# A four-layer streaming encoder step on eight cores: layer order, folded pool matrix, and the convolution as banded matmuls

## The chip, the cores and the metric

The kernel runs on all 8 cores of one Trainium2 chip. Each core computes one prompt stream of 4096 frames and four of 32 short streams of 32 frames; the cores exchange nothing. The time is the device time of the slowest core, in microseconds (us). The runs here fall into two states. In the fast one all cores agree within about 1%. In the slow one the cores of a die, or of both, show a lower granted TensorE clock and run some per cent longer (in the slow run of the kernel after one die took 4432.5 to 4500.5 us at clock 0.845 to 0.847, the other 4151.3 to 4173.9 us at 0.939 to 0.942).

## The reference

The model is 1024 wide, each branch 2048. Four layers: pool, conv, gating, pool.

```python
def rmsnorm(x, g): ...
def pool_mixer(u, hist, offset, w_grp, scale):
    # trailing-window means over 2, 4, 8, 16 frames, one window per 512 channels
    ...
    d = mean - u
    y = jnp.einsum('btgc,gcd->btgd', d, w_grp).reshape(B, T, E) * scale   # 512x512 group matrix
def conv_mixer(a, hist, w, b, ng, nb):
    # causal depthwise convolution, 31 taps, then LayerNorm and silu
    ...
def sgu_mixer(u, v, ws, bs, ng, nb):
    # LayerNorm of v, lower-triangular mix over 128 positions per head, y = u * s
    ...
for i in range(4):                      # pool, conv, gating, pool
    h = rmsnorm(x, norm_g[i])
    p = h @ in_w                        # 2E columns for pool, 3E for the others
    ...                                 # y = mixer(...)
    x = x + (y * jax.nn.silu(z)) @ out_w
return rmsnorm(x, final_g), ...         # and the last history rows of each layer
```

## The kernel before

It takes a group of 512 tokens (four of the eight groups carry 32 sample tokens too) through all four layers before it takes the next, and streams all weights from DRAM in each pass:

```python
for g in range(ngroups):                # 8 passes
    load_x(g)
    pool_layer(G, g, ...)
    conv_layer(G, g, ...)
    sgu_layer(G, g, ...)
    pool_layer(G, g, ...)
    rmsnorm(...)                        # final norm, store
```

The first pass loads each weight tile as f32 and casts it on ScalarE; it then stores the bf16 tile for the later passes:

```python
if grp == 0:
    S.add("sp", lambda e: [e.dma_start(out=stg[:, st, :], in_=wst[ci])], ...)
    S.add("act", lambda e: e.activation(out=slots[:, sl, :], in_=stg[:, st, :], func=AF.Copy), ...)
    S.add("act", lambda e: [e.dma_start(out=wq[ci], in_=slots[:, sl, :])], ...)
else:
    S.add("sp", lambda e: [e.dma_start(out=slots[:, sl, :], in_=wq[ci])], ...)
```

The convolution is split by taps. TensorE takes 19 of them (`NPE`), each as a matmul with a 128x128 diagonal; VectorE takes 12 as multiply-adds on the accumulator (the first of them, not shown, also fetches TensorE's sum from PSUM; the loop below does the other eleven):

```python
for k in range(NPE):                                   # pe_taps: TensorE
    for bi, (c0, n) in enumerate(cblocks):
        inst = e.matmul(psap(tAcc, bi, n), lhsT=dg[:, ...], rhs=agb[:, p, k + c0:k + c0 + n], ...)
...
ks = list(range(NPE + 1, 31))                          # rest: VectorE
for i, k in enumerate(ks):
    for ct in cts:
        S.add("dve", lambda e: e.scalar_tensor_tensor(
            out=big[:, ct, 0:Wc], in0=seqb[:, q, k:k + Wc], scalar=wcol,
            in1=big[:, ct, 0:Wc], op0=ALU.mult, op1=ALU.add), ...)
```

Of the kernel before, what the change touches and what calls it, by code (L numbers as in the profile page):

```python
# [11 lines left out]
D = 1024  # L12
# [5 lines left out]
TP = 512  # L18
NG = SEQ // TP
NCH = 120  # L20
NSLOT = 9
PF = 6
# [3 lines left out]
BIGW = 512 + 30 + 32  # L26
SEQW = 512 + 60 + 32

P_NORMG = 0
P_FINALG = P_NORMG + 32  # L30
P_PSCALE = P_FINALG + 8
P_CONVW = P_PSCALE + 32
P_CONVB = P_CONVW + 496
P_CONVNG = P_CONVB + 16
P_CONVNB = P_CONVNG + 16
NPAR = P_CONVNB + 16
B_SGG = 0
B_SGB = B_SGG + 2048
B_BSB = B_SGB + 2048
B_MASK = B_BSB + 512  # L40
B_RATIO = B_MASK + 128
B_IDENT = B_RATIO + 64
NBC = B_IDENT + 128
PINGPONG = True
NPE = 19

class Op:
    __slots__ = ("eng", "fn", "deps", "mark", "markno", "dkey", "dval", "idx", "tag")

class Sched:  # L50
    def __init__(self):
        self.ops = []
        self.last_w = {}
        self.readers = {}
        self.dcount = {}
        self.tag = None

    def add(self, eng, fn, reads=(), writes=(), dkey=None, ndma=1):
        op = Op()
        op.eng, op.fn, op.mark, op.markno, op.dkey, op.dval = eng, fn, False, 0, dkey, 0  # L60
        op.idx = len(self.ops)
        op.tag = self.tag
        deps = set()
        for k in reads:
            w = self.last_w.get(k)
            if w is not None:
                deps.add(w)
        for k in writes:
            w = self.last_w.get(k)
            if w is not None:  # L70
                deps.add(w)
            for r in self.readers.get(k, ()):
                deps.add(r)
        wset = set(writes)
        for k in writes:
            self.last_w[k] = op
            self.readers[k] = []
        for k in reads:
            if k not in wset:
                self.readers.setdefault(k, []).append(op)  # L80
        deps.discard(op)
        op.deps = deps
        if dkey is not None:
            self.dcount[dkey] = self.dcount.get(dkey, 0) + ndma
            op.dval = 16 * self.dcount[dkey]
        self.ops.append(op)
        return op

def build_program(depth=4, ngroups=NG):
    nc = bass.Bass("TRN2", target_bir_lowering=False)  # L90
    S = Sched()

    def dram(name, shape, dt, kind):
        return nc.dram_tensor(name, shape, dt, kind=kind).ap()

    xT = dram("xT", [8, 128, SEQ + NSAMP * SLEN], F32, "ExternalInput")
    wst = dram("wst", [NCH, 128, 2048], F32, "ExternalInput")
    params = dram("params", [128, NPAR], F32, "ExternalInput")
    bcin = dram("bcin", [128, NBC], F32, "ExternalInput")
    sgwT = dram("sgwT", [128, 4, 128], F32, "ExternalInput")  # L100
    stpool = dram("stpool", [2, NSAMP, 128, 240], F32, "ExternalInput")
    stconv = dram("stconv", [NSAMP, 128, 480], F32, "ExternalInput")
    yT = dram("yT", [8, 128, SEQ + NSAMP * SLEN], F32, "ExternalOutput")
    o_poolp = dram("o_poolp", [2, 128, 240], F32, "ExternalOutput")
    o_pools = dram("o_pools", [2, NSAMP, 128, 240], F32, "ExternalOutput")
    o_convp = dram("o_convp", [128, 480], F32, "ExternalOutput")
    o_convs = dram("o_convs", [NSAMP, 128, 480], F32, "ExternalOutput")
    o_sgup = dram("o_sgup", [128, 2048], F32, "ExternalOutput")
    o_sgus = dram("o_sgus", [NSAMP, SLEN, 2048], F32, "ExternalOutput")
    wq = dram("wq", [NCH, 128, 2048], BF16, "Internal")  # L110
    dgq = dram("dgq", [16, 128, NPE * 128], BF16, "Internal")

    es = ExitStack()

    def sb(name, shape, dt):
        return es.enter_context(nc.sbuf_tensor(name, shape, dt))

    ps = es.enter_context(nc.psum_tensor("ps", [128, 4096], F32))
    x = sb("x", [128, 8, 544], F32)
    h = sb("h", [128, 8, 544], BF16)  # L120
    ym = sb("ym", [128, 16, 544], BF16)
    big = sb("big", [128, 16, BIGW], F32)
    slots = sb("slots", [128, NSLOT, 2048], BF16)
    stg = sb("stg", [128, 2, 2048], F32)
    par = sb("par", [128, NPAR], F32)
    bc = sb("bc", [128, NBC], F32)
    sgw32 = sb("sgw32", [128, 4, 128], F32)
    wmT = sb("wmT", [128, 4, 128], BF16)
    ones_d = sb("ones_d", [128, 128], BF16)
    ones_e = sb("ones_e", [128, 128], BF16)  # L130
    epsb = sb("epsb", [128, 2], F32)
    pool_hp = sb("pool_hp", [128, 2, 16, 15], F32)
    conv_hp = sb("conv_hp", [128, 16, 30], F32)
    st_pool = sb("st_pool", [128, 2, 240], F32)
    st_conv = sb("st_conv", [128, 480], F32)
    pso = sb("pso", [128, 2, 240], F32)
    cso = sb("cso", [128, 480], F32)
    seqb = sb("seqb", [128, 4, SEQW], F32)
    sA = sb("sA", [128, SEQW], F32)
    sB = sb("sB", [128, SEQW], F32)  # L140
    dbuf = sb("dbuf", [128, 4, 544], BF16)
    dbuf2 = dbuf[:, :, :].rearrange("p a b -> p (a b)")
    t32 = sb("t32", [128, 2, 544], F32)
    t16 = sb("t16", [128, 2, 544], BF16)
    rs = sb("rs", [128, BIGW], F32)
    vraw = sb("vraw", [128, 2048], F32)
    bst = sb("bst", [128, 2, 24], F32)
    agb = sb("agb", [128, 2, SEQW], BF16)
    ident_bf = sb("ident_bf", [128, 128], BF16)
    ym2d = ym[:, :, :].rearrange("p a b -> p (a b)")  # L150
    DGOFF = [0, 5 * 544]
    dg = ym2d
    stg2d = stg[:, :, :].rearrange("p a b -> p (a b)")
    DGK = [[("ym", c) for c in range(0, 5)], [("ym", c) for c in range(5, 10)]]
    assert NPE * 128 <= 5 * 544
    dgs = vraw[:, :].bitcast(BF16)
    vrawB = ym2d[:, 0:4096].bitcast(F32)
    vnbB = ym2d[:, 4096:6144]
    assert tuple(vrawB.shape) == (128, 2048), vrawB.shape
    mv = sb("mv", [128, 2, 4], F32)  # L160

    state = {"tile": 0, "loaded": 0, "par": 0, "fine": 0}

    def next_tile(G):
        n = len(G["tiles"])
        t = state["tile"] % n
        state["tile"] = (t + 1) % n
        return G["tiles"][t]

    def psap(tile, bi, n, p0=0, p1=128, off=0):  # L170
        b = tile[bi]
        return ps[p0:p1, b * 512 + off: b * 512 + off + n]

    def PK(tile):
        return [("psb", b) for b in tile]

    def gstruct(g):
        even = (g % 2 == 0)
        if even:
            return dict(T=544, segs=[(0, 512), (512, 32)], blocks=[(0, 272), (272, 272)], s=g // 2,  # L180
                        tiles=[(0, 1), (2, 3), (4, 5)], aux=(6, 7), xi=0, g=g)
        return dict(T=512, segs=[(0, 512)], blocks=[(0, 512)], s=None,
                    tiles=[(b,) for b in range(7)], aux=(7,), xi=(1 if PINGPONG else 0), g=g)

    def XAP(G, k, c0, n):
        if G["xi"] == 0:
            return x[:, k, c0:c0 + n]
        return stg2d[:, k * 512 + c0:k * 512 + c0 + n]

    def XK(G, k):  # L190
        return ("x", k) if G["xi"] == 0 else ("xo", k)

    def pieces(G, c0, n, H):
        out = []
        for si, (s0, sn) in enumerate(G["segs"]):
            lo, hi = max(c0, s0), min(c0 + n, s0 + sn)
            if lo < hi:
                seqoff = H + (0 if si == 0 else 512 + H) + (lo - s0)
                cloff = (0 if si == 0 else 512 + H) + (lo - s0)
                out.append((lo, hi - lo, seqoff, cloff))  # L200
        return out

    def issue_load(gi):
        ci = gi % NCH
        grp = gi // NCH
        sl = gi % NSLOT
        if grp == 0:
            st = gi % 2
            S.add("sp", lambda e, ci=ci, st=st: [e.dma_start(out=stg[:, st, :], in_=wst[ci])],
                  reads=[], writes=[("stg", st)], dkey=("stg", st))  # L210
            S.add("act", lambda e, st=st, sl=sl: e.activation(out=slots[:, sl, :], in_=stg[:, st, :], func=AF.Copy),  # L211
                  reads=[("stg", st)], writes=[("slot", sl)])
# [5 lines left out]

    total_chunks = ngroups * NCH

    def use_chunk(gi, hold_from=None):
        upto = min(gi + PF, total_chunks - 1)
        if hold_from is not None:
            upto = min(upto, hold_from + NSLOT - 1)
# [862 lines left out]
```

## Time and profile before

| | before |
|---|---|
| runs | 5867.57, 5870.03 (fast), 6044.85, 6302.73 (slow) |
| TensorE busy | 4602 us, 78% |
| VectorE busy | 3348 us, 57% |
| granted TensorE clock, by core's die | 0.889 and 0.888 |

"Busy" for TensorE includes matmuls at half clock, so it is not work at the full rate: on core 7, the slowest, the 3.20 us from 1240.7 us on, at a granted clock of 0.50, touch 9 matmuls of 512 columns, the 3.40 us from 1244.1 us on, at 1.00, touch 18.

### The profile page before, as it was taken

The numbers are of one execution on the slowest core, as the hardware profiler recorded it, in microseconds if no ns is written. First come the engines' busy times: TensorE is split into PE (matmuls) and PEld (weight loads), VectorE is DVE, ScalarE is ACT, GpSimd is POOL, SyncE is SP. The second block draws the span as 40 slices with busy tenths as digits, with TensorE's granted clock in tenths as the row PEclk, the third lists the DMA queues.
The fourth block names the chain that finished last, engine by engine and source line by source line (L and its number), as shares of the span: only waits on it lengthen the run. The fifth ranks groups of instructions, "written<-read, shape, count | busy, mean of one in ns | idle before, by whom it ended". The sixth has DMA issues, their size and how long they took to land.

```text
span 5874.6 us, 89444 instructions; the slowest of 8 cores (5853.6 to 5874.6 us)
## 1 busy us (share of the span) xinstructions
PE 4602.0 (78%) x28896; PEld 2847.9 (48%) x28896; DVE 3348.4 (57%) x5365; ACT 1642.2 (28%) x3070; POOL 914.8 (16%) x1632
## 2 busy tenths in 40 slices
PE   3576667687898778987898878888798867998787
PEld 2454445233446556632436656733345646753343
DVE  2357415466465863658455765558646585466745
ACT  4434344213122142213222131221322122221312
POOL 3302011001111111201112121200112011210110
PEclk7787889898999889998999889999899979999888
DMA  6564587332443214432344222343243312443232
GB/s 223 216 219 129 172 290 245 130 117 77 136 142 117 83 60 148 140 120 85 113 148 138 98 79 96 127 143 109 86 148 133 113 62 92 140 138 123 90 114 97
DMA packets 208039, 768.82 MB, mean 131 GB/s; under 512 B 30432, under 2 KB 33888, under 8 KB 191840
## 3 DMA queue, kind: packets, MB, share of 16 engines
q1 hardware_dynamic: 188000, 690.23, 36.3%
q10 hardware_dynamic: 19584, 72.88, 3.0%
q8 instruction: 242, 3.96, 0.3%
q14 instruction: 213, 1.74, 0.1%
HBM read 668.29 MB, written 94.73 MB: 130 GB/s over the span
## 4 chain that ended last, share of the span: by engine, by line
PE 49%; DVE 19%; issue 13%; ACT 8%; DMA 6%; POOL 3%; ACTq 0%; DVEq 0%; SPq 0%; POOLq 0%
PE ps L242 30%; PE ps L513 11%; DMA stg<-wst 5%; DVE big L540 3%; PE ps L254 3%; PE ps L698 2%; DVE rs L290 2%; ACT slots L211 2%; DVE sA L375 2%; DVE sB L380 1%; DVE sA L384 1%; PE ps L306 1%; POOL ym L652 1%; DVE dbuf L400 1%; DVE h L292 1%
## 5 line engine op out<-in xcount | busy, mean ns | idle before, releaser
L242 PE MATMUL ps<-h,slots 128*128 128x272 bf16 (+1 forms) x13056 | 2031.0, 316 | 265.9 <-ACT big L413 112.3
L242 PEld LDWEIGHTS ps<-h,slots 128*128 128x128 bf16 x13056 | 1280.9, 99 | 994.7 <-issue 313.9
L540 DVE SCALAR_TENSOR_TENSOR big<-seqb,par,big 128x574 f32<-128x574 f32 (+1 forms) x1408 | 987.8, 782 | 0.0
L513 PE MATMUL ps<-agb,ym 128*128 128x287 bf16 (+1 forms) x3648 | 663.8, 349 | 205.4 <-ACT agb L489 201.2
L242 PE MATMUL ps<-ym,slots 128*128 128x272 bf16 (+1 forms) x5376 | 809.3, 313 | 2.2 <-DVE x L314 2.2
L242 PEld LDWEIGHTS ps<-ym,slots 128*128 128x128 bf16 x5376 | 525.2, 98 | 280.5 <-issue 3.2
L513 PEld LDWEIGHTS ps<-agb,ym 128*128 128x128 bf16 x3648 | 383.0, 106 | 485.6 <-issue 279.6
L365 ACT ACTIVATE seqb<-ps 128x272 f32<-128x272 f32 (+3 forms) x512 | 172.4, 392 | 760.1 <-PE ps L242 231.5
L423 DVE SCALAR_TENSOR_TENSOR ym<-ps,par,big 128x272 bf16<-128x272 f32 (+1 forms) x384 | 212.5, 582 | 297.2 <-PE ps L242 287.6
L369 POOL COPY pool_hp<-seqb 128x15 f32<-128x15 f32 x256 | 151.5, 592 | 1436.9 <-ACT seqb L365 1436.9
L698 PE MATMUL ps<-slots,h 128*128 128x256 bf16 (+1 forms) x2304 | 278.6, 286 | 91.8 <-DVE h L292 91.8
L791 DVE TENSOR_TENSOR t<-ps,t 128x272 f32<-128x272 f32 (+1 forms) x192 | 94.7, 522 | 438.2 <-ACT t L788 438.2
L794 POOL TENSOR_TENSOR ym<-t,big 128x544 bf16<-128x544 f32 (+1 forms) x128 | 154.7, 1209 | 1185.9 <-DVE t L791 1185.9
L314 DVE TENSOR_TENSOR x<-ps,x 128x272 f32<-128x272 f32 x256 | 100.4, 436 | 403.2 <-PE ps L242 310.7
L242 PE MATMUL ps<-dbuf,slots 128*128 128x272 bf16 (+1 forms) x1536 | 261.3, 330 | 79.4 <-DVE dbuf L400 76.7
L467 ACT ACTIVATE t<-ps 128x272 f32<-128x272 f32 (+1 forms) x192 | 82.1, 462 | 855.2 <-PE ps L242 855.1
L254 PE MATMUL ps<-h,slots 128*128 128x272 bf16 (+1 forms) x768 | 211.7, 424 | 136.8 <-DVE h L292 118.9
L375 DVE TENSOR_TENSOR sA<-seqb 128x573 f32<-128x573 f32 (+1 forms) x256 | 187.2, 731 | 206.6 <-ACT seqb L365 194.6
L698 PEld LDWEIGHTS ps<-slots,h 128*128 128x128 bf16 (+1 forms) x2304 | 234.5, 102 | 132.1 <-issue 94.0
L652 POOL TENSOR_TENSOR ym<-big,t 128x512 bf16<-128x512 f32 x192 | 207.3, 1107 | 495.3 <-ACT big L644 492.8
L211 ACT ACTIVATE slots<-stg 128x2048 bf16<-128x2048 f32 x120 | 229.5, 1912 | 172.3 <-DMA stg<-wst 162.1
L314 DVE TENSOR_TENSOR stg<-ps,stg 128x512 f32<-128x512 f32 x128 | 88.0, 691 | 327.3 <-PE ps L242 288.5
(97 smaller groups left out, 4146.6 us busy)
## 6 DMA issues: line engine op xcount, KB each, us to landing
slots<-wq SPq DMA_DIRECT2D x840, 512.0 KB, 3.8
stg<-wst SPq DMA_DIRECT2D x120, 1024.0 KB, 8.1
ym<-dgq SPq DMA_DIRECT2D x128, 608.0 KB, 4.1
wq<-slots ACTq DMA_DIRECT2D x120, 512.0 KB, 8.1
yT<-big SPq DMA_DIRECT2D x64, 256.0 KB, 3.0
dgq<-vraw ACTq DMA_DIRECT2D x16, 608.0 KB, 2.8
x<-xT SPq DMA_DIRECT2D x32, 256.0 KB, 5.5
stg<-xT SPq DMA_DIRECT2D x32, 256.0 KB, 2.8
```

Source lines behind the costliest of these rows:

```text
L211: S.add("act", lambda e, st=st, sl=sl: e.activation(out=slots[:, sl, :], in_=stg[:, st, :], func=AF.Copy), reads=[("stg", st)], writes=[(" ...
L242: inst = e.matmul(psap(tile, bi, n), lhsT=lhs_fn(k), rhs=rhs_fn(k, c0, n), start=(k == 0), stop=(k == nk - 1))
L254: inst = e.matmul(psap(tile, bi, n), lhsT=slots[:, sl, k * 256 + m2 * 128: k * 256 + m2 * 128 + 128], rhs=h[:, k, c0:c0 + n], start=(k == ...
L314: blockwise("dve", G, lambda e, bi, c0, n, m=m, tile=tile: e.tensor_tensor(out=XAP(G, m, c0, n), in0=psap(tile, bi, n), in1=XAP(G, m, c0, ...
L365: inst = e.activation(out=seqb[:, p, so:so + ln], in_=psap(tile, bi, ln, off=lo - c0), func=AF.Copy)
L375: S.add("dve", lambda e, p=p: e.tensor_tensor(out=sA[:, 1:W], in0=seqb[:, p, 1:W], in1=seqb[:, p, 0:W - 1], op=ALU.add), reads=[("seqb", p ...
L423: blockwise("dve", G, lambda e, bi, c0, n, ct=ct, tile=tile: e.scalar_tensor_tensor(out=ym[:, ct, c0:c0 + n], in0=psap(tile, bi, n), scala ...
L513: inst = e.matmul(psap(tAcc, bi, n), lhsT=dg[:, DGOFF[p] + k * 128:DGOFF[p] + (k + 1) * 128], rhs=agb[:, p, k + c0:k + c0 + n], start=(k = ...
L540: S.add("dve", lambda e, q=q, ct=ct, wcol=wcol, k=k: e.scalar_tensor_tensor(out=big[:, ct, 0:Wc], in0=seqb[:, q, k:k + Wc], scalar=wcol, i ...
L652: inst = e.tensor_tensor(out=ym[:, ct, lo:lo + ln], in0=big[:, ct, co:co + ln], in1=t32[:, p, lo:lo + ln], op=ALU.mult)
L698: inst = e.matmul(psap(tile, bi, 256, p0=0, p1=nt, off=c2 * 256), lhsT=h[:, k, tok0:tok0 + nt], rhs=slots[:, slv[cc], k * 256:(k + 1) * 25 ...
L794: S.add("pool", lambda e, p=p, ct=ct: e.tensor_tensor(out=ym[:, ct, 0:T], in0=t32[:, p, 0:T], in1=big[:, ct, 0:T], op=ALU.mult), reads=[(" ...
```

## The change

The intent: go layer by layer over all tokens with x and h in DRAM between the layers, so that the norm of one group lies beside the matmuls of another; fold the pool's group matrix into the input weights; let TensorE do the whole convolution with few columns; drop ScalarE's weight casts by letting the DMA cast; and let a list scheduler choose the order on each engine. The diff, cut to its core:

```diff
-for g in range(ngroups):
-    pool_layer(...); conv_layer(...); sgu_layer(...); pool_layer(...)
+self.phase("A"); self.pool_layer(0, 0)
+self.phase("B"); self.conv_front()
+self.phase("C"); self.conv_back()
+self.phase("D"); self.sgu_layer()
+self.phase("E"); self.pool_layer(1, 3)
...
+def load_chunk(self, name, t):
+    if ("wq", name) in S.last_w:      # a bf16 copy exists: plain load
+        S.add("sp", lambda e: e.dma_start(out=t.ap(BF16), in_=w), ...)
+    else:                             # f32 in DRAM, bf16 in SBUF: cast in the DMA
+        S.add("pool", lambda e: e.dma_start(out=t.ap(BF16), in_=w), ...)
+def precast(self, name, after=()):    # cast copy DRAM to DRAM, for later layers
+    op = S.add("pool", lambda e: e.dma_start(out=dst, in_=src), ...)
...
+# conv_front: 32x32 block transpose of the product, then banded matmuls over blocks of 32 frames
+S.add("dve", lambda e: e.transpose(
+    T.ap(BF16)[:, 0:32 * NBLK].rearrange("p (c b) -> p b c", b=NBLK)[:, b0:b0 + nb, :],
+    G.ap(BF16)[:, 0:32 * nb].rearrange("p (b t) -> p b t", t=32)), ...)
+...
+for half in range(2):
+    r = e.matmul(p.ap()[:, i * NB:(i + 1) * NB], lhsT=W[:, ...],
+                 rhs=Ta[:, c, 1 - half:1 - half + NB], start=(half == 0), stop=(half == 1))
+...
+# conv_back: the multiply by silu(z) on GpSimd
+S.add("pool", lambda e: e.tensor_tensor(out=o..., in0=y..., in1=z..., op=ALU.mult), ...)
```

Two of these ideas need a word. The window mean of a pool layer acts on frames and its group matrix on channels, so the order can be swapped and the product of the input weights and the group matrix made once ("folding"); only the last 15 rows of the branch, an output, still need the weights as they were (the "last rows"). For the convolution the transpose lays the 32 frames of a block across partitions, so that the 31 taps of a channel become a 32x32 band matrix; two matmuls, for this block and the one before, with one column for each of 136 blocks, do four channels at once.

## The prediction

> **What bounds the kernel now.** I read the page of the slowest core first: busy times, slices, and the summary of the chain that ended last.
>
> ```profile
> span 5874.6 us, 89444 instructions; the slowest of 8 cores (5853.6 to 5874.6 us)
> PE 4602.0 (78%) x28896; PEld 2847.9 (48%) x28896; DVE 3348.4 (57%) x5365; ACT 1642.2 (28%) x3070; POOL 914.8 (16%) x1632
> ...
> PE   3576667687898778987898878888798867998787
> DVE  2357415466465863658455765558646585466745
> ...
> PEclk7787889898999889998999889999899979999888
> DMA  6564587332443214432344222343243312443232
> ...
> PE 49%; DVE 19%; issue 13%; ACT 8%; DMA 6%; POOL 3%; ACTq 0%; DVEq 0%; SPq 0%; POOLq 0%
> ```
>
> No engine is full: TensorE is busy 78% and half of the chain is TensorE; the rest is VectorE, waits for issue, ScalarE and DMA. The slices show why: TensorE is at 3 to 7 tenths in the first seven, and later a dip comes back where VectorE's 8 stands. PEclk falls in the same slices. Then the spans of the dies, and busy times by stretch: the first ms, the rest, two stretches without a gap, and the three mixers of one 512-token pass (pool, conv, gating), cut where the timeline of matmuls changes its source lines. Columns: length, TensorE, weight loads, VectorE, ScalarE, GpSimd (busy us, instructions), granted clock, DMA share, GB/s.
>
> ```profile
> die 0 (median of its cores): 5860.3 us, clock 0.889
> die 1 (median of its cores): 5865.3 us, clock 0.888
> ```
>
> ```profile
> 0.00:1000.00 1000.00, 605.72 (x4527) 449.38 (x4528) 430.84 (x772) 446.76 (x713) 193.58 (x401) 0.83 0.63 215
> 1000.00:5874.00 4874.00, 3996.28 (x24371) 2398.52 (x24369) 2917.58 (x4593) 1195.44 (x2357) 721.25 (x1231) 0.90 0.35 114
> 1520.00:1590.00 70.00, 70.00 (x326) 31.74 (x325) 14.53 (x21) 12.21 (x21) 18.39 (x17) 1.00 0.54 164
> 3610.00:3685.00 75.00, 75.00 (x636) 60.97 (x634) 15.77 (x40) 13.53 (x34) 17.68 (x16) 1.00 0.45 139
> 3826.00:3937.00 111.00, 102.27 (x458) 45.08 (x456) 65.41 (x89) 25.48 (x43) 13.04 (x33) 0.96 0.52 164
> 3937.00:4201.00 264.00, 206.41 (x853) 85.31 (x853) 189.18 (x258) 71.35 (x110) 34.92 (x46) 0.87 0.31 101
> 4201.00:4348.00 147.00, 123.42 (x716) 69.54 (x715) 68.57 (x130) 28.54 (x48) 18.98 (x17) 0.92 0.38 122
> ```
>
> Three things follow. First, the rate: 326 records touch 70 us, about two of them only at an edge, so a 512-column matmul costs 70/324 = 216 ns; with 636 records in 75 us a 272-column one costs 118 ns. Second, conv takes 264 us where its 856 matmuls of 512 columns need 856 x 0.216 = 185; VectorE is busy 189 of the 264. Pool takes 111 (need 456 x 0.216 = 98), gating 147 (need about 120). Third, the first ms has a granted clock of 0.83 and 215 GB/s: weights come in as f32 and pass through a ScalarE cast. Now the costly groups:
>
> ```profile
> L242 PE MATMUL ps<-h,slots 128*128 128x272 bf16 (+1 forms) x13056 | 2031.0, 316 | 265.9 <-ACT big L413 112.3
> L540 DVE SCALAR_TENSOR_TENSOR big<-seqb,par,big 128x574 f32<-128x574 f32 (+1 forms) x1408 | 987.8, 782 | 0.0
> L513 PE MATMUL ps<-agb,ym 128*128 128x287 bf16 (+1 forms) x3648 | 663.8, 349 | 205.4 <-ACT agb L489 201.2
> L211 ACT ACTIVATE slots<-stg 128x2048 bf16<-128x2048 f32 x120 | 229.5, 1912 | 172.3 <-DMA stg<-wst 162.1
> ```
>
> The convolution is done twice over: 3648 TensorE matmuls for 19 taps (each a 128x128 diagonal) and 1408 VectorE instructions, 988 us, for most of the other 12 taps. At gap-free rates all 28896 matmuls need: 14912 of 272 columns x 0.118 = 1760; 8672 of 512 x 0.216 = 1873; 2432 of 287 x 0.122 (scaled) = 297; 2304 of 256 x 0.110 (scaled) = 253; 576 small x 0.058 = 33; together 4216 us. So about 1650 of the 5870 us are gaps and half-clock time. In the clock records only 1.0 and 0.5 occur.
>
> [...]eight cores run the same program and gap-free stretches of 45 to 75 us stand at 1.00. [...]the 128x512 multiply by the norm factor, beside a GpSimd multiply, takes 1490 ns against about 690 elsewhere. [...]
>
> **The change, part by part.** The order of instructions of both kernels gives exact counts. Columns streamed by TensorE:
> before 9,851,520. Diagonal taps go: -2432x287 - 1216x512 = -1,320,576. The group matmuls go: -1024x272 - 512x512 = -540,672. The four sample streams share one gating block: -49,152. Added: folding 256x512 = 131,072; banded taps 1024x136 = 139,264; last history rows 64x512 = 32,768; small ones 8,192. After: 8,252,416, 16% less, in 18,681 matmuls, because prompt groups are all 512 wide and the samples are one group of 128.
>
> By stage, gap-free (216 ns, 56 ns, 60 ns for 136 columns):
> - A, first pool layer: 8 groups x 400 x 0.216 = 691; sample group 400 x 0.056 = 22; folding 128 x 0.216 = 28; last rows and history 9: 750 us.
> - B, conv front: 2048 x 0.216 + 256 x 0.056 + 1024 x 0.060 = 517.
> - C, conv back: 8 x 296 x 0.216 + 296 x 0.056 + folding 28 + 2 = 558.
> - D, gating: 1056 x 0.216 + 528 x 0.056 + 8 x 392 x 0.216 + 392 x 0.056 = 957.
> - E, last pool layer: 8 x 392 x 0.216 + 22 + 7 = 706.
> Sum 3488, against 4216: 728 us less work for TensorE.
>
> What stands beside it. VectorE in B: the 988 us of taps become per channel tile and group one product (0.69) and two 32x32-block transposes (unknown, I assume 0.7 each): 8.25 x 2.1 + issue gaps = 19 us beside 32 us of TensorE per tile. ScalarE there: sigmoids 5, copies of banded results 11 x 0.5, band building 16 x 0.63: 21 us. Both hidden. The ScalarE casts of weights (120 x 1.9 us) go; the cast is in the DMA. In the pool layers VectorE is close. The timeline of the kernel before, in a tile of window 16 (start, length, then the instruction):
>
> ```profile
> 4420.72 0.70 DVE L384 TENSOR_TENSOR sA<-sB 128x520 f32<-128x520 f32 x1
> 4421.52 0.69 DVE L388 TENSOR_TENSOR sB<-sA 128x512 f32<-128x512 f32 x1
> 4422.33 0.69 DVE L400 SCALAR_TENSOR_TENSOR dbuf<-sB,seqb 128x512 bf16<-128x512 f32 x1
> 4422.94 0.70 DVE L375 TENSOR_TENSOR sA<-seqb 128x526 f32<-128x526 f32 x1
> ```
>
> A step that needs the one before starts 0.81 us later, an independent one 0.61. In the new kernel a tile's chain is sums, difference, gate product, each needing the last: windows 2, 4, 8, 16 cost about 2.3, 3.1, 3.9, 4.7 us, against 16 x 0.216 = 3.46 us of TensorE. Four tiles each: 56 us; with 8 residual adds (0.64), 8 norm products (0.68) and a 3.4 us reciprocal, 70 us of the 85. But in windows 8 and 16 VectorE needs 34.4 us where TensorE needs 27.7, and only three u tiles of buffer lie between: about 6 us lost per group. Waits moved away: by going layer by layer, the norm of one group hides behind another's matmuls, where now each norm stops TensorE 6.5 to 11 us, five times a pass.
>
> Additions for each stage over its gap-free time: A +100 (start 25 until the first h, VectorE lag 50, weights and casts 25): 850. B +43: 560. C +92, because per 64 us of TensorE it has about 60 of ScalarE and 50 of VectorE with GpSimd conflicts: 650. D +33: 990. E +74, and 15 for the last norm and store: 795. Four changes of layer, with half clock after them: 35. Sum 850+560+650+990+795+35 = 3880 us.
>
> **Rivals.**
> 1. VectorE or ScalarE becomes the bound of a stage. For: 70 of 85 us in the pool layers before any disturbance, and a static order planned with shorter durations than the trace shows (0.61 planned for a sum, 0.70 measured, no gap for a dependent step). If the transposes, strided on one side, take 1.4 us instead of 0.7, B's VectorE needs about 31 us per tile and B grows by 40 to 100. If the pool layers run at VectorE's pace with 15% more, +150. Time then 4050 to 4200.
> 2. DMA and the GpSimd queue bound stage A. 68 cast loads of 1 MB, 49 cast copies DRAM to DRAM of 1.5 MB, 34 MB of x in, 17 out, weights: about 25 MB per group of 90 us, 275 GB/s, where the first ms before reached 293 GB/s in its best 100 us. [...] Against: the copies are ahead of need by a layer. Cost 50 to 250: 3930 to 4130.
> 3. The denser TensorE is throttled. For: a slow state exists (6045 us)[...]. Against: 1.00 in dense stretches of all cores. [...]
> 4. Everything hides as planned: 3488 + start and end 60 + layers 35: about 3600.
>
> **Range and chances.** The centre takes partial losses in A, C and E. The low end is rival 4; the high end has rivals 1 and 2 together, or part of 3: 3600 to 4300. [...] only a failure outside all this gives same or slower: faster 0.98, same 0.01, slower 0.01.
>
> **What would show it.** Right: TensorE busy above 90% with the clock at 0.95 or more, a chain mostly TensorE, VectorE at 60 to 70%, no tap instructions, 512-column matmuls each 216 ns, ScalarE free of 2048-wide casts at the start, stage ends near 850, 1410, 2060, 3050. Wrong: a clock between 0.5 and 1.0 in records (rival 3); slices at the start with DMA at 9 and TensorE below 6 (rival 2); VectorE at 9 tenths in pool or conv-front slices, transposes above 1 us (rival 1).

## More of the kernel before

`arena` in the profile after is the one block of memory in which a pool allocator places nearly all tiles; `ps` is PSUM, `wst` the f32 weights, `wq` their bf16 copies, `hd` the h of the next layer, `yd` the result of the convolution, all four in DRAM.

## The result and the profile after

The kernel after took 4177.66 us (median of 4; three fast runs of 4172.0 to 4181.14, one slow of 4502.07). The ratio to before is 0.711, 95% interval 0.7094 to 0.7126. Ratios here are the mean time of one kernel's fast runs over that of the other's fast runs of the same rounds, so they are not quite the ratio of the medians quoted. The time lies inside the predicted range, 298 us above the centre.

The page of the kernel after, its slowest core: span, TensorE busy, then TensorE, its clock and the DMA engines in 40 slices, and the chain of work that ended last:

```profile
span 4179.6 us, 58691 instructions; the slowest of 8 cores (4148.8 to 4179.6 us)
...
PE 3614.8 (86%) x18339; PEld 1720.5 (41%) x18681; DVE 2568.2 (61%) x3551; ACT 1608.5 (38%) x2677; POOL 504.9 (12%) x887
...
PE   6996888884997997797886799999999989999996
...
PEclk9998999997999998898998899999999999999998
DMA  7655666579886668566656735666556763233224
...
PE 63%; DVE 16%; DMA 8%; issue 6%; ACT 3%; POOL 2%; SPq 1%; DVEq 0%; ACTq 0%; POOLq 0%
```

TensorE's busy time fell by 987 us (4602 to 3615) and its idle time by 708 (5875 - 4602 = 1273 to 4180 - 3615 = 565): that is the whole 1695. By the prediction's counts 728 of the 987 are fewer columns at full rate. The other 259 are the difference; I put them down to less time at half clock, as the mean granted clock rose from 0.89 to 0.94. (342 of the 18681 matmuls are missing from the trace after, so its busy time is a little low.) "issue" in the chain, time in which nothing visible was awaited, fell from 13% to 6%.

The dips of the first line tell where the rest is lost: the first 10 slices and slices 16 to 22. Cut at the first and last instruction of each stage, core 2 gives these rows (start and end, length, then busy us of TensorE, its weight loads, VectorE, ScalarE and GpSimd with their instructions, then the clock, the DMA share and GB/s); they are stages A to E:

```profile
0.00:1054.00 1054.00, 823.63 (x3913) 377.53 (x3984) 656.15 (x959) 322.00 (x556) 168.32 (x409) 0.90 0.68 147
1054.00:1608.00 554.00, 506.32 (x3100) 268.26 (x3161) 498.62 (x431) 302.93 (x539) 22.83 (x55) 0.96 0.73 200
1608.00:2368.00 760.00, 594.18 (x2815) 270.38 (x2866) 351.06 (x489) 429.02 (x733) 217.28 (x154) 0.89 0.63 201
2368.00:3361.00 993.00, 952.84 (x4866) 457.43 (x4959) 511.86 (x836) 317.99 (x448) 0.20 (x1) 0.99 0.61 197
3361.00:4180.00 819.00, 737.82 (x3654) 346.93 (x3715) 550.50 (x839) 236.52 (x403) 96.24 (x268) 0.96 0.33 110
```

A is idle for 230 us and C for 166; together they hold 70% of the 565. D shows what the plan can do: 953 busy of 993 at clock 0.99.

The table compares this with the prediction. A ends here at the first banded matmul, so it holds the first channel tile of B; by the prediction's own counts that tile is (128 x 0.216 + 16 x 0.056) = 29 us, and I have moved them from B to A. Measured values are means of the eight cores of the profiled run, with their range.

| stage | predicted | measured | off by |
|---|---|---|---|
| A first pool layer | 879 | 1035 (1015 to 1054) | +156 |
| B conv front | 531 | 555 (549 to 564) | +24 |
| C conv back | 650 | 760 (754 to 766) | +110 |
| D gating | 990 | 995 (988 to 1001) | +5 |
| E last pool layer | 795 | 819 (817 to 820) | +24 |
| layer changes | 35 | in the stages | -35 |
| sum | 3880 | 4164 | +284 |

What TensorE waited for in A on core 2 (line, releaser, total us, times, longest; those below 20 us are left out):

```profile
PE ps L608 <- DMA arena<-wst: 40.1, 7, 15.7
PE ps L608 <- DMA arena<-wq: 38.5, 3, 22.9
PE ps L638 <- ACT arena L632: 36.5, 9, 22.5
PE ps L889 <- DMA arena<-wst: 30.2, 3, 23.1
PE ps L696 <- DVE arena L858: 25.2, 7, 4.4
PE ps L608 <- DMA arena<-hd: 22.4, 5, 15.2
```

Four of six lines are DMA: weights with a cast (`wst`), bf16 weights that the first layer had folded and stored (`wq`), and at the end of A the last-rows weights (L889) and h. They make 131 us on this core. On the other three of the longer A (cores 0, 4, 6) it is 115 to 128, on the four of the shorter (1, 3, 5, 7) 86 to 98. L638 is the norm at the start, L858 VectorE's gate product in the pool layer. Two rows of the DMA issues, with their median time to landing:

```profile
arena<-wq SPq DMA_DIRECT2D x474, 512.0 KB, 4.3
...
arena<-wst POOLq DMA_DIRECT2D x104, 512.0 KB, 12.0
```

A casting load brings the same 512 KB into SBUF, and its median is nearly three times as long. But these medians mix stages: most casting loads lie in A, most plain ones later. In A on core 2 the 20 plain loads land after 12.5 us and the 73 casting ones after 13.6; in B it is 4.2 and 6.4. The traffic in A explains more of the gap than the cast does. In C the two largest waits of TensorE are these:

```profile
PE ps L696 <- POOL arena L1154: 106.5, 10, 18.7
PE ps L1119 <- ACT arena L1113: 25.7, 26, 7.6
```

L1154 is the multiply by silu(z) on GpSimd, L1113 a ScalarE instruction of the LayerNorm. The groups by shape (busy us, mean ns, then idle before them) show the cost of that multiply, and of the transposes in B:

```profile
L1028 DVE STREAM_TRANSPOSE arena<-arena 128x512 bf16<-128x512 bf16 x128 | 313.5, 2449 | 11.1 <-DVE arena L1002 0.5
...
L1080 DVE STREAM_TRANSPOSE arena<-arena 128x512 f32<-128x512 f32 x128 | 136.2, 1098 | 23.7 <-DMA yd<-arena 23.6
...
L1146 DVE TENSOR_TENSOR arena<-arena 128x512 f32<-128x512 f32 x128 | 89.0, 765 | 0.8
```

```profile
L1154 POOL TENSOR_TENSOR arena<-arena 128x512 bf16<-128x512 f32 x128 | 203.7, 1630 | 423.9 <-ACT arena L1148 423.9
```

In E one wait dominates, on the same VectorE product as in A:

```profile
PE ps L696 <- DVE arena L858: 44.1, 16, 4.6
```

### The profile page after: what moved, and what is told of

Its sections match the earlier page's. It is cut to its first block, busy times and chain, and to the rows that moved or that the text cites. A ratio compares the mean times of both kernels' runs of the same rounds, so it can differ in the third digit from the quotient of the medians.

```text
span 4179.6 us, 58691 instructions; the slowest of 8 cores (4148.8 to 4179.6 us)
## 1 busy us (share of the span) xinstructions
PE 3614.8 (86%) x18339; PEld 1720.5 (41%) x18681; DVE 2568.2 (61%) x3551; ACT 1608.5 (38%) x2677; POOL 504.9 (12%) x887
## 3 DMA queue, kind: packets, MB, share of 16 engines
q0 software_dynamic: 17024, 88.09, 13.3%
## 4 chain that ended last, share of the span: by engine, by line
PE 63%; DVE 16%; DMA 8%; issue 6%; ACT 3%; POOL 2%; SPq 1%; DVEq 0%; ACTq 0%; POOLq 0%
PE ps L608 31%; PE ps L696 21%; DVE arena L833 6%; PE ps L1243 5%; DMA arena<-wq 3%; DVE arena L654 3%; DMA arena<-wst 2%; DVE arena L647 2%; DVE arena L843 2%; PE ps L638 2%; POOL arena L1154 2%; DVE arena L1146 1%; DMA yd<-arena 1%; PE ps L1067 1%; PE ps L747 1%
## 5 line engine op out<-in xcount | busy, mean ns | idle before, releaser
L608 PE MATMUL ps<-arena 128*128 128x512 bf16 (+1 forms) x10151 | 2144.7, 366 | 192.3 <-DMA arena<-wq 54.6
L608 PEld LDWEIGHTS ps<-arena 128*128 128x128 bf16 x10368 | 970.5, 99 | 1241.5 <-issue 240.6
L696 PE MATMUL ps<-arena 128*128 128x512 bf16 (+1 forms) x4526 | 1001.0, 374 | 186.3 <-POOL arena L1154 106.5
L696 PEld LDWEIGHTS ps<-arena 128*128 128x128 bf16 x4608 | 443.7, 101 | 700.1 <-issue 253.9
L700 DVE TENSOR_TENSOR arena<-ps,arena 128x512 f32<-128x512 f32 (+1 forms) x288 | 185.3, 646 | 773.2 <-PE ps L696 706.1
L833 DVE TENSOR_TENSOR arena<-arena 128x526 f32<-128x526 f32 (+4 forms) x720 | 476.1, 661 | 105.6 <-ACT arena L811 58.5
L632 ACT ACTIVATE arena<-arena 128x512 bf16<-128x512 f32 (+1 forms) x360 | 208.1, 591 | 749.9 <-DVE arena L700 716.0
L1028 DVE STREAM_TRANSPOSE arena<-arena 128x512 bf16<-128x512 bf16 (+1 forms) x144 | 334.2, 2321 | 11.1 <-DVE arena L1002 0.5
L1154 POOL TENSOR_TENSOR arena<-arena 128x512 bf16<-128x512 f32 (+1 forms) x144 | 212.0, 1510 | 467.8 <-ACT arena L1148 467.8
L849 ACT ACTIVATE arena<-ps 128x512 f32<-128x512 f32 (+1 forms) x288 | 161.5, 561 | 223.7 <-PE ps L608 202.4
L858 DVE SCALAR_TENSOR_TENSOR arena<-arena 128x512 bf16<-128x512 f32 (+1 forms) x288 | 204.3, 709 | 48.7 <-DVE arena L843 40.7
L1243 PE MATMUL ps<-arena 128*128 128x512 bf16 x1035 | 228.6, 379 | 4.4 <-DMA arena<-wq 3.2
L654 DVE SCALAR_TENSOR_TENSOR arena<-arena 128x512 bf16<-128x512 f32 (+3 forms) x360 | 226.7, 702 | 5.3 <-DVE arena L647 1.6
L1327 ACT ACTIVATE arena<-ps 128x512 f32<-128x512 f32 (+1 forms) x144 | 80.7, 562 | 377.2 <-PE ps L608 377.0
L1330 DVE TENSOR_TENSOR arena<-ps,arena 128x512 f32<-128x512 f32 (+1 forms) x144 | 92.9, 645 | 171.7 <-PE ps L608 138.8
```

The lines of the kernel that those rows point to most:

```text
L608: r = e.matmul(P[:, 0:T], lhsT=W[:, k * 256 + base:k * 256 + base + 128], rhs=H[:, k * 512:k * 512 + T], start=(k == 0), stop=(k == 7))
L632: self.S.add("act", lambda e: e.activation(out=q.ap(BF16)[:, 0:T], in_=xt[k].ap()[:, 0:T], func=AF.Square), reads=[xt[k]], writes=[q], cos ...
L654: self.S.add("dve", lambda e, k=k: e.scalar_tensor_tensor(out=(h.ap(BF16)[:, k * 512:k * 512 + T] if h is not None else xt[k].ap()[:, 0:T] ...
L696: r = e.matmul(P[:, 0:T], lhsT=W[:, k * 128:(k + 1) * 128], rhs=ym[k].ap(BF16)[:, 0:T], start=(k == 0), stop=(k == 15))
L700: S.add("dve", lambda e, t=t, m=m: e.tensor_tensor(out=xt[m].ap()[:, 0:T], in0=t.ap()[:, 0:T], in1=xt[m].ap()[:, 0:T], op=ALU.add), reads= ...
L833: return e.tensor_tensor(out=V(dst, lo, n), in0=V(src, lo, n), in1=V(src, lo - step, n), op=ALU.add)
```

## The experiments

Twelve kernels ran. Two more ideas could not be built: the change with program order instead of the list scheduler, and row blocks of the output projection between the tiles of A as well; in both the tile allocator deadlocked. So the scheduler's own share, and that of the layer order alone, stay open.

### The multiply of conv back on VectorE (a_dve_mul)

```diff
-        S.add("pool", lambda e: e.tensor_tensor(... op=ALU.mult), reads=[y, z], writes=[o], cost=c_pool(T))
+        S.add("dve", lambda e: e.tensor_tensor(... op=ALU.mult), reads=[y, z], writes=[o], cost=c_tt(T))
```

> The gate multiply of the conv back stage (ym = y x z, 128 of 128x512, 1.63 us each on GpSimd, one behind the other) is moved to VectorE; nothing else is edited. Stage C lasts 760 us from the last banded matmul to the first gating value matmul, against 558 gap-free, and the out projection there waits 106 us for GpSimd. Theory (GpSimd's serial multiplies are what ends each group of C): each group's 12 us wait goes, C falls by 70 to 110 us, total near 4080. Rival (ScalarE with its silus, squares and table loads ends C, GpSimd only comes last): the wait moves to ScalarE or VectorE and the total changes by less than 30 us. VectorE's own 128x512 multiply in C should fall from 765 ns to about 690 in both.

Median 4139.47 us, ratio to before 0.7041 (0.7023 to 0.7058) against 0.711. C fell from 760 to 706 us (mean of cores), the other stages by no more than 2. The multiply takes 682 ns on VectorE, and VectorE's other multiply fell from 765 to 685. TensorE's wait in C:

```profile
PE ps L696 <- DVE arena L1154: 52.7, 12, 10.3
```

The gain in C, 54 us, is below the expected 70 to 110: it is half of the 110 by which C missed its prediction, and a quarter of its 202 over gap-free. The total fell by 38, more than the rival allowed. The rest stays: TensorE's output projection now waits for VectorE at the end of the chain norm product, silu on ScalarE, multiply.

### Weight copies in A spread out (a_spread)

```diff
-            self.pool_cts(j, g, h, range(2, 8), ym)
-            ...self.precast_some(4)
-            self.pool_cts(j, g, h, range(8, 16), ym)
-            ...self.precast_some(3)
+            for c in range(2, 16, 2):          # cut: the norm of the next group stays before tile 8
+                self.pool_cts(j, g, h, range(c, c + 2), ym)
+                self.precast_some(1)
```

> In stage A the casting copies DRAM to DRAM that prepare later layers' weights are issued one after each pair of channel tiles, where they come as bursts of 4 and 3; their number is the same. Stage A lasts 1054 us to the first banded matmul, of which I predicted about 885 with one tile of B in it. TensorE waits there about 130 us in all for weight or h transfers whose landing takes 12 to 24 us instead of 4 to 12. Theory (bursts of copies stand in front of urgent loads): A falls by 40 to 70 us, total near 4120. Rival (the amount of bytes, or the GpSimd queue's order, is what delays): A changes by less than 20 us.

Median 4213.86 us, ratio 0.7178: slower. A rose from 1035 to 1063. That the copies come in bursts is not the harm; this theory fell. The rival's "less than 20 us" was passed too, by 8; why spreading them costs time is open.

### Output projection in row blocks in E (a_mix)

```diff
-            self.pool_cts(j, g, h, range(0, 2), ym)
-            self.pending_out()                     # all eight row blocks of the group before
+            steps = self.outproj_steps(lay, pg, pym, wn)
+            for c in range(0, 16, 2):              # last pool layer only
+                self.pool_cts(j, g, h, range(c, c + 2), ym)
+                next(steps, None)                  # one row block
```

> Only in the last pool layer (stage E) the out projection of the group before is cut in its eight row blocks and one is placed after each pair of channel tiles, instead of all eight after the first pair. Work is the same. Theory (VectorE lags in windows 8 and 16, where a tile costs it 3.9 and 4.7 us against TensorE's 3.46, and the out projection then waits 5.5 us a group for the last gate products): TensorE gets 10.4 us of work per pair for 8.5 to 10 us of VectorE, the 44 us of waits in E go, E falls from 819 to 770 to 785, total 35 to 50 us less. Rival (VectorE's total of 70 us per 85, plus the norm and its semaphore waits, is too much wherever it lies): the waits appear elsewhere in E and the total changes by less than 15 us.

Median 4143.55 us, ratio 0.7063. E fell from 819 to a mean of 785 (772 to 786 on six cores, 806 and 815 on cores 6 and 7, whose die has a mean granted clock of 0.931 to 0.936 where the other has 0.945 to 0.948). The wait on L858 is gone. VectorE's lag behind TensorE in windows 8 and 16 is real, and work in between hides it.

### The transposed buffer block by block (a_transp), and in pairs (a_tr2)

The transpose writes 2-byte elements, in the kernel after each 274 bytes from the one before. `a_transp` makes its writes contiguous; the banded matmul then reads its columns at a step of 64 bytes.

```diff
-    T...rearrange("p (c b) -> p b c", b=NBLK)[:, b0:b0 + nb, :]
+    T...rearrange("p (b c) -> p b c", c=32)[:, b0:b0 + nb, :]
```

> The buffer of block transposes in the conv front is laid out block by block instead of channel by channel: the transpose writes whole rows (64 contiguous bytes) and the banded matmul reads its 136 columns with a step of 64 bytes. The transposes took 2.45 us each against 0.7 assumed; VectorE is 47 of 50 us busy in B. Theory (the strided 2-byte writes make the transpose slow and VectorE bounds B): the transpose falls to 0.7 to 1.1 us, VectorE to under 70% in B, B falls from 554 us towards 500 to 520, total 35 to 50 us less. Rival (TensorE pays for its strided read what VectorE saves): banded matmuls take 120 to 200 ns instead of 60 and B stays or grows. Second rival (the transpose itself needs 2.4 us for 2-byte data whatever the layout): nothing changes.

Median 4282.91 us, ratio 0.7289: slower, B 670 instead of 555. The rival came, and larger than its 120 to 200 ns: on core 1 TensorE is now busy 665 of B's 670 us, VectorE only 304. `a_tr2` keeps two neighbouring channels together, so VectorE writes 4 bytes at a time and the matmul reads at a step of 4 bytes:

```diff
-    T...rearrange("p (c b) -> p b c", b=NBLK)[:, b0:b0 + nb, :]
+    T...rearrange("p (c b r) -> p b c r", b=NBLK, r=2)[:, b0:b0 + nb, :, :]
...
-    rhs=Ta[:, c, 1 - half:1 - half + NB]
+    rhs=Ta[:, c // 2, 1 - half:1 - half + NB, c % 2]
```

> The kernel after with the transposed buffer laid out in pairs of channels: VectorE then writes runs of 2 neighbours (4 bytes) instead of single elements, and the banded matmul reads its columns at a step of 4 bytes instead of 2. If the transpose costs by the number of separate runs written, it takes about half of 2449 ns, some 1.3 us, and the matmul stays near 60 ns gap-free; stage B loses 20 to 50 us, the whole is 4125 to 4165. Rival 1: a step of 4 bytes already slows the matmul as the step of 64 did (there about 113 ns more per matmul): B rises. Rival 2: writes below some larger run cost the same each, so the transpose stays at 2.4 us: within 0.5% of after.

Median 4139.84 us, ratio 0.7047; B 506. VectorE is busy 300 of B's 503 us on core 2, where it was 499 of 554: it did bound B. The timelines of TensorE show the matmuls themselves (start, us, then the group). First `a_transp`, then `a_tr2`:

```profile
1204.23 1.55 PE L1067 MATMUL ps<-arena 128*128 128x136 bf16 x6
1205.60 3.63 PE L608 MATMUL ps<-arena 128*128 128x512 bf16 x16
```

```profile
1204.03 0.54 PE L1067 MATMUL ps<-arena 128*128 128x136 bf16 x6
1204.40 3.62 PE L608 MATMUL ps<-arena 128*128 128x512 bf16 x16
```

From start to start, six banded matmuls take 1.37 us, 228 ns each, in the first, and 0.37 us, 62 ns each, in the second. That is 166 ns x 1024 = 170 us more for `a_transp`, of which B gets back the 30 us of waits for the transpose and some gaps. And the transpose of `a_tr2`:

```profile
L1028 DVE STREAM_TRANSPOSE arena<-arena 128x512 bf16<-128x512 bf16 x128 | 90.7, 708 | 11.1 <-DVE arena L1002 0.5
```

The expected size was wrong in the good direction: two neighbours already bring it down to what contiguous writes take (707 ns), not to half. Why two neighbours are enough no run isolates.

### No weight copies in A (a_defer)

```diff
-            if first:
-                self.precast_some(4)
...
-            if first:
-                self.precast_some(3)
...
-            self.precast_some(2)       # per channel tile of B
+            self.precast_some(5)
```

> The kernel after with no cast copies of weights from DRAM to DRAM in stage A (first pool layer); they are issued five per channel tile at the start of conv front instead of two. The same bytes move in the end. My theory for A's extra 170 us: the copies (49 in A by plan, 10.7 to 12.0 us each to landing, about 3.3 us of all 16 DMA engines each) lie in the queues before the weight loads that TensorE waits for. Then A falls by 40 to 100 us on all four looked-at cores and B, with little else on its DMA, rises by less than 25: the whole is 4080 to 4150. Rival 1: A is held by its own casting loads (68 of 1 MB) and by VectorE, not by the copies: A stays within 30, the whole within 1% of after. Rival 2: the burst in B makes its transposed-band work or its weights late: B rises by what A gains, or more.

Median 4286.02 us, ratio 0.7291: slower than after. A fell by 46, from 1035 to 989 us, as the theory said; on core 2 TensorE's waits for weights there fell from 109 us (40.1, 38.5 and 30.2) to 12, and those for h from 22.4 to 12.6. Plain loads in A landed after 6.1 us instead of 12.5, casting ones after 10.2 instead of 13.6. The gain is smaller than the waits that went, because another took their place, VectorE's gate product, which had been 25.2 us (54 to 59 on all cores now):

```profile
PE ps L696 <- DVE arena L858: 58.2, 16, 4.4
```

So the DMA hid part of VectorE's lag in A, and taking all its waits away would not give all of their time back. And B rose by 149, which was the second rival. In B the loads of h landed late:

```profile
arena<-hd SPq DMA_DIRECT2D x38, 1024.0 KB, 22.7
```

In the kernel after it is 8.1 us there; the DMA share of B rose from 0.73 to 0.87, and the waits lay on ScalarE and VectorE, which stood behind late loads and stores. B had too little slack in DMA for five copies per tile: 49 copies cost 46 us in A and 149 in B.

### The taps of the kernel before (b_nodve, b_notaps)

Their outputs are wrong, which doesn't matter for the times.

```diff
 # b_nodve, and b_notaps too:
-                for ct in cts:
+                for ct in ():                 # no VectorE taps in rest()
 # b_notaps only:
-                for k in range(NPE):
+                for k in (0, NPE - 1):        # 2 of 19 diagonals
```

> The kernel before with VectorE's twelve conv taps left out (a wrong result on purpose; TensorE's 19 taps stay). It asks what bound the conv stage of the kernel before, whose steady pass took 264 us with VectorE busy 189 of them and TensorE needing 185. If VectorE's taps bound it, the conv stage falls to 190 to 230 us, 35 to 75 a pass, and the whole by 280 to 600 us: 5280 to 5600. Rival: TensorE with its own gaps (the norm, the mean sums, waits for ScalarE) bounds it, VectorE's taps are beside it: the whole falls by less than 120 us, above 5760.

> The kernel before without VectorE's taps and with 2 of TensorE's 19 diagonal taps (a wrong result on purpose). By gap-free counts the 17 taps left out of 19 are 1,320,576 x 17/19 = 1,181,568 columns, [...]500 us in all. If TensorE binds the conv stage once VectorE's taps are gone, the whole falls by 400 to 550 us more than in the run without VectorE's taps: 4800 to 5150. That would be what the whole change of the convolution could win at most, and what is left of the 1700 us would belong to the order of layers, the group matrix and the loads. Rival: what is beside it (ScalarE, norm, weights from DRAM) takes over, and the fall is under 300 us more.

The edit leaves out eleven of VectorE's taps, not twelve as the expectation says: the twelfth (L527), which fetches TensorE's sum from PSUM, is not in the loop. `b_nodve` took 5500.26 us in its profiled fast run; the fast ratio is 0.9407 (0.9294 to 0.9521). Against fast runs of before (5873 to 5878) this is 373 us or a little more, 47 per pass, inside the expected 35 to 75. TensorE's diagonals before had waited 205.4 us, mostly for a copy on ScalarE (L489); in the trace of before that copy itself waited 114.6 us for VectorE's product (L481), which stood in VectorE's queue behind the taps. Without the taps the diagonals wait less than half as long:

```profile
L513 PE MATMUL ps<-agb,ym 128*128 128x287 bf16 (+1 forms) x3621 | 572.0, 316 | 94.8 <-ACT agb L489 93.5
```

`b_notaps` had one run fast (5227.09, but with cores 4 and 5 at clock 0.872 and 0.873, where cores 0 to 3 have 0.897 and 0.898) and five slow. In the five runs in which one die was undisturbed, its cores took 5116 to 5136 us. Compared with 5478 to 5502 of undisturbed dies in `b_nodve` this is 365 less, below the expected 400 to 550 and above the rival's 300; the 500 us of work (498 at 216 ns for 512 columns) did not all come back. The 28 taps left out of 31 were worth about 740 of the 1700 us together, before the new convolution pays for itself. If gains add, the larger part is not the convolution; how it splits among layer order, group matrix, loads and scheduler no run shows.

### The parts that helped, together (c_combo, c_back, c_late)

`c_combo` is `a_dve_mul`, `a_mix` and `a_tr2` in one. `c_back` adds a store of each weight tile of the first layer that was loaded with a cast, so that repeats are plain loads:

```diff
             S.add("pool", lambda e: e.dma_start(out=t.ap(BF16), in_=w), writes=[t], ...)
+            if name[0] in ("z", "o") and name[1] == 0:
+                dst = self.wq[WQ[name]]
+                S.add("sp", lambda e: e.dma_start(out=dst, in_=t.ap(BF16)), reads=[t], writes=[("wq", name)], ...)
```

`c_late` is `c_combo` with fewer copies in A and B and the last ones in C:

```diff
-                self.precast_some(3)          # A, second half of a group
+                self.precast_some(1)
...
-            self.precast_some(2)              # B, per channel tile
+            self.precast_some(1)
...
+                if ct in (6, 12):             # C
+                    self.precast_some(1)
```

> The kernel after with the three edits that helped each alone: the conv multiply on VectorE (38 us of the whole), the last pool layer's output projection cut in row blocks between the tiles (34 us), the transposed buffer in pairs (38 us). They lie in three stages, C, E and B, so if the stages simply add, the whole is 4178 - 110 = 4068 us, range 4055 to 4085, with A near 1045, B near 505, C near 708, D near 995, E near 773. Rival: a gain in one stage is taken back in the next (the order is planned anew for the whole program, and buffers shift): above 4090.

> The combined version, and in the first pool layer a weight tile that was loaded with a cast is also stored once as bf16, so that its later loads are plain 512 KB loads from the fast queue, not 1 MB casting loads through GpSimd. My theory for what is left of A's extra time after the copies (about 59 us): the 68 casting loads, half of them repeats, hold the GpSimd queue and the DMA engines, so that the waits for loads in A fall: A is 20 to 60 us shorter than in the combined version. Rival 1: the repeats come with time to spare and A's gaps are the start, VectorE's lag behind TensorE in the output projection and the loads of the stage's end: A stays within 12. Rival 2: the added stores (16 of 512 KB) collide with x loads and A grows.

> The combined version with 5 instead of 7 weight copies per group in A, one instead of two per channel tile in B, and the last 13 in conv back, where GpSimd has nothing left to multiply. If the copies' cost in A is by number (49 cost 59 us, 1.2 each), 14 fewer there are worth about 17 us; B then carries 16 instead of 15 over twice as many tiles and should stay within 8, C within 8. The whole falls by 10 to 20 against the combined version. Rival: B is as touchy as when all were put there (150 us for 49 more, 3 us each, because its own transposed-band stores and loads share the queues), and C too: no gain or a loss of up to 30.

Only one of seven runs of before was fast (5870.65), so no interval is given, and the three are compared with each other by the means of three fast runs each.

| | median | mean of fast | A | B | C | D | E |
|---|---|---|---|---|---|---|---|
| c_combo | 4054.46 | 4052.6 | 1031 | 507 | 712 | 995 | 778 |
| c_back | 4031.6 | 4030.2 | 1013 | 509 | 712 | 999 | 778 |
| c_late | 4052.04 | 4049.5 | 1020 | 496 | 737 | 998 | 779 |

The three edits add up, even 14 us beyond the 4068 expected. `c_back` gains 22 us more, of which A shows 18 (mean; 1050 to 1023 on its slowest core): just below the theory's 20 to 60, above the rival's 12. `c_late` wins 11 in A and 11 in B and loses 25 in C: the rival. (Its expectation counts 59 us for the 49 copies; the mean of `a_defer` over eight cores is 46.) `c_back` gives the right result, is the fastest seen, and lies 3.5% under the kernel after (mean of fast runs 4175.8). It was run at another time. TensorE is busy for 90% of its span:

```profile
PE 3623.6 (90%) x18681; PEld 1715.4 (43%) x18681; DVE 2428.3 (60%) x3695; ACT 1605.7 (40%) x2676; POOL 284.0 (7%) x711
```

### The late loads at the end of A (a_lastz)

The last-rows matmul of the first layer takes weights that the layer uses anyway. Its output is wrong, which doesn't matter for the time.

```diff
-            w = self.chunks([("un", j, 2 * q + i) for i in range(2)])
+            w = self.chunks([("z" if j == 0 else "un", j, 2 * q + i) for i in range(2)])
```

> The kernel after, in which the last-rows matmul at the end of the first pool layer takes its weights from tiles that the layer uses anyway (a wrong result on purpose; the same instructions on TensorE and VectorE, six casting loads fewer near the end of A). The waits of TensorE from 900 to 1060 us showed 30 us for these loads and 22 us for the loads of h of the next layer. If the eight late weight loads are a cost of their own, A's mean over the eight cores falls from 1035 to 995 to 1010 us, and the whole by 25 to 40, to 4138 to 4153. Rival: the DMA engines are full at this point (0.93 of them busy) and what follows, h and the conv taps, is as late: A falls by less than 12 or B's start takes it back, and the whole stays within 0.3%.

Two fast runs, 4159.8 and 4172.38 us, three slow. A fell from 1035 to 1013 (998 to 1034), 22 us, between theory and rival. On core 2 the wait for these weights (30.2 us) is gone and that for h rose from 22.4 to 26.4. The whole changed by 10 us in the mean of fast runs, about as much as single fast runs differ, so I take A's 22 us as shown and the gain in the whole as unclear.

## Why the prediction was right or wrong

**Work at full rate: right.** In the timeline of `a_tr2` 16 matmuls of 512 columns take 3.46 us from start to start, 216 ns each; 16 of 128 columns on core 2 of the kernel after take 0.90 us (3342.57 to 3343.47 us), 56 ns each; and D, which had the smallest allowance, came out at 995 for 990.

**A: the step that failed is the term "weights and casts 25" of the allowance of 100.** TensorE's DMA waits in A were 131 us on the core looked at, 86 to 131 over all cores. Of the excess of 156 the experiments show 46 for the copies for later layers, 18 for repeated casting loads, and 22 for the late last-rows loads, 86 if they add, which was not tried together. The prediction had this as its second rival, with 50 to 250 us, and put 25, half of its low end, into the centre. The other two terms were near: 36.5 us at the norm for "start 25", and 25.2 us (and 14.4 for VectorE's copies of the folded weights) for "VectorE lag 50"; with the copies gone, in `a_defer`, that lag shows as 58. The wait is also paid twice, since TensorE works at half clock after it: after the 22.9 us for `wq` its busy 3.98 us from 360.3 to 364.5 us, at a granted clock of 0.50, hold 10 matmuls of 512 columns, and the busy 10.35 us from 364.6 to 375 us, at 1.00, hold 49. In A 72 us of TensorE's busy time lie in clock records of 0.5 (mean clock 0.90), and its busy time is 824 us where 750 + 29 are needed, 45 more. About 70 us of A's excess therefore rest on waits that no experiment took away.

**C: "+92" was half the size needed; the "GpSimd conflicts" in it were small, and GpSimd's own multiply was missing from it.** The excess over the gap-free 558 was 202. Moving the multiply took 54 of it. I had counted GpSimd only as a disturber of VectorE; in fact its own 1630 ns, 16 x 1.63 = 26 us per group, stood at the end of a chain which the output projection waits for. What it cost VectorE was 80 ns on each of 128 multiplies (765 ns in the mean, 685 with GpSimd's multiply gone), 10 us. What remains, some 150 us over gap-free, waits for VectorE and ScalarE, which the prediction named; how it splits is open.

**B: transposes "0.7 each" were wrong, the sum nearly right.** They took 2449 and 1098 ns. Per tile VectorE has then 8.25 x (0.69 + 2.45 + 1.10) = 35 us beside 32 of TensorE, and it was busy 499 of the 554 us: rival 1's bound. B exceeded its 531 by only 24, and the run in pairs gives back 49 and lands below the prediction. That B came out near is partly luck: rival 1 gave 40 to 100 us for transposes of 1.4 us, and these were longer.

**E: "about 6 us lost per group" was right.** The wait was 44.1 us over eight groups, 5.5 each, and taking it away was worth about 41 (819 to 778 in `c_combo`).

**Rivals.** Rival 3 did not come: all 846 clock records of the eight cores in the kernel after are 0.5 or 1.0. Its one slow run took 4502 us, with a die at 0.845 to 0.847. Rival 4 fell short as 565 us of idle stayed. Rivals 1 and 2 both came in part, which is why the time is above the centre, as the range allowed.

**Signs.** TensorE above 90% busy: no, 86%. Clock 0.95 or more: no, 0.938 to 0.942. Slices with DMA at 9 and TensorE below 6: only slice 10, the end of A (DMA 9, TensorE 4); in the nine before DMA stands at 5 to 7. Slices would have cleared the DMA for most of A; the waits of TensorE did not. ScalarE without 2048-wide weight casts: yes. Of the signs of rival 1, transposes above 1 us came (2449 and 1098 ns), and VectorE stands at 9 tenths in two slices of B. Stages ended at about 1006, 1590, 2350 and 3346 us where 850, 1410, 2060 and 3050 were given. The prediction's "done twice over" is a slip: 19 taps and 12 taps are a split, as its own counts have it.

## What to carry to other kernels

Moving a cast into the DMA does not make it free (landing after 6.4 us instead of 4.2 in B, 13.6 instead of 12.5 in A): count the landing time, the issuing queue and what urgent load stands behind it, and look for the stage that still has DMA slack before moving transfers there. A reordering that leaves TensorE waiting pays twice where the granted clock falls too (A: 45 us more busy time than the counts need). A wait that is taken away can uncover the one behind it, so read the waits again after each edit (`a_defer`). Small pieces of independent work put between dependent tiles (a row block of the output projection) hid VectorE's lag better than one large block (E: 819 to 785 us). When a layout serves two engines, try a small run of elements (two were enough here: 708 ns for the transpose, 62 ns for the matmul) before giving one side contiguous access.

## What these runs measured of the hardware

- Steps of a layout: a 128x512 bf16 transpose on VectorE took 2449 ns with single elements written at 274 bytes, 708 ns with pairs, 707 ns contiguous; a 136-column matmul took 228 ns with its moving operand at a step of 64 bytes, 62 ns at 4. The f32 transpose back, which reads single elements 544 bytes apart and writes them contiguously, took 1098 ns.
- Granted clock: in the traces of the kernels before and after all records of the eight cores, 2062 and 846, are 0.5 or 1.0, and core 2 of the kernel after is 96% busy for the 993 us of D at 0.99. In the slow `b_notaps` the mean of core 6 from 3400 to 3500 us is 0.79 with TensorE 98% busy, where core 1 has 0.90 and is 84% busy; from 4400 to 4500 us they stand at 0.76 and 0.77, from 2400 to 2500 us both at 0.91 (each core's time is counted from its own first instruction). What brings the lower clock on these runs do not settle. From 3406.88 us on 48 matmuls of 512 columns take 12.78 us on core 6, 266 ns each, more than the 216 at 1.00 and less than at 0.50, where 8 take 3.60 us (from 963.77 us on core 2 of the kernel after):

```profile
3406.88 12.78 PE L242 MATMUL ps<-h,slots 128*128 128x512 bf16 x48
```

- Casts in the DMA: in A on core 2 a casting load of 512 KB landed after 13.6 us (median) and a plain one after 12.5, without the copies (`a_defer`) after 10.2 and 6.1, in B after 6.4 and 4.2; the 168 casting transfers of the kernel after, all issued from GpSimd, held 13.3% of all DMA engines, 13.3% x 4180/168 = 3.3 us of all sixteen for each.
- VectorE beside GpSimd: in the kernel before 52 of the 64 multiplies of 128x512 by the norm factor start while GpSimd is busy and take 1676 ns in the mean, the other 12 take 688. In the kernel after 78 of 128 do and take 818, the other 50 take 684; the mean fell from 765 to 685 ns when GpSimd's multiply was gone.
